# Denominators as extra columns of v, weight casts held behind the heads' norms, and three low parts on GpSimd

## The chip, the cores and the metric

The kernel runs on one core of a Trainium2 chip. The metric is the device time of one execution in microseconds. A profile of one execution is read beside it: the matmul engine (TensorE, PE), the vector engine (VectorE, DVE), the activation engine (ScalarE, ACT), GpSimd (POOL) and the queue that issues DMAs (SyncE, SP) are recorded instruction by instruction.

## The reference

Two layers of a decoder trunk on 256 tokens of width 1024. Each layer has a token mixer, a residual with layer norm, a SwiGLU channel mixer, a second residual with layer norm, and a gated embedding. Layer 0 mixes tokens with a gated spatial unit, layer 1 with an mLSTM block of 4 heads, each 512 wide. The change lies in layer 1. What matters of it:

```python
q, k = headwise_linear(xc, w_q), headwise_linear(xc, w_k)
v = headwise_linear(xm, w_v)
...
s = einsum('bhtd,bhsd->bhts', qb, kb) * exp(dmat - m_t[..., None])
num = einsum('bhts,bhsd->bhtd', s, vb) + ...
den = sum(s, axis=-1) + ...
h = num / maximum(abs(den), exp(-m_t))[..., None]
...
h = layer_norm(h, norm_g).reshape(B, S, ML_INNER) + skip * xc
return (h * silu(z)) @ w_out
```

So each head needs its weighted sum of v, the plain sum of its scores (the denominator), a division, and a layer norm over its 512 columns. The result is scaled, added to a skip path, gated by silu(z) and multiplied by the output weights.

## The kernel before

**Two parts for each number.** All products run in a reduced fp32 format, and each operand is split in a high part (a rounded copy) and a low part (the rest). A product is then three matmuls: high by high, low by high, high by low. `split` (L150) makes the parts: ScalarE copies the high one, and `sub`, VectorE unless the call says GpSimd, subtracts for the low one.

**Weights.** They stream from HBM in blocks of 128x1024 in the order of a list. `ahead` (L169 on) issues loads into four "raw" buffers and casts raw blocks into six "w" buffers, two instructions a block, so many blocks ahead of the block in use. A raw buffer is free again when both parts are made. The output weights are the blocks ("mo", 0) to ("mo", 15). `behind["cast"]` holds instructions that later casts are to be ordered behind: `issue_after` puts such an order only between instructions of the same engine, as an order in that engine's queue and not as a wait on another engine.

**Order of the work.** A planner puts each engine's instructions in an order before the run: of those that are ready by its own estimate, the one that comes first in the program. At run time each engine takes its queue strictly in that order. Only the ScalarE instructions of the gate stage stand in program order, by hand.

**The mLSTM stage.** Every head h has four blocks of 128 features. First come the products for xm, q and v (L754 to L797); v goes, in two parts, into one buffer `vn[h]` (L726, L796). Then scores (L801 to L824), then gates and exponentials, which end in the weights of the sums, `phi` (high) and `plo` (low, made on GpSimd), for every head (L896 to L914). Because of causality a head has three 128x128 blocks of them: one for the first 128 tokens, two for the second 128.

Then `pv_block(h)` (L923): nine matmuls of 512 columns add up the weighted sum for both token halves in two PSUM banks of pool A (`num`), and six matmuls against ones, two columns each, add up the denominators in a bank of pool B (`pd`). Each pool has four banks. VectorE forms 1/max(|den|, .) (L944 to L948), statistics of num (L952, L953), the variance (L956); GpSimd raises it to -1/2 (L957, "pow"); VectorE makes the scale and the shift, `nb` (L958, L960); ScalarE applies both while it reads num from PSUM (L962), and the banks are free.

`h_block(h)` (L967) transposes a head's result on TensorE and lets VectorE and ScalarE make its four features: scale and skip (L976), gate (L977), and the two parts.

The order in the program is: for each head, `pv_block`, then one block of z (24 matmuls of 256 columns); `h_block(0)` behind z of head 2; then `h_block(1)` and the product with the output weights. That product accumulates over 16 features into four banks of pool A, two for each token half (t = 0, 1). The first three features are taken together, all of t = 0 and then all of t = 1; later ones one by one.

## Time and profile before

| what | value |
|---|---|
| median of 3 runs | 823.44 us (823.26 to 823.69) |
| profiled execution | 823.71 us |
| its span in the trace | 822.0 us |
| TensorE matmul busy | 816.2 us (99%) |
| VectorE busy | 616.9 us (75%) |
| ScalarE busy | 471.8 us (57%) |
| GpSimd busy | 152.1 us (19%) |
| granted TensorE clock | 0.999 |

The heads' sums start at 535.1 us of the span and the product with the output weights at 559.0 us. A row of a timeline gives the start, the length (of several, if merged: x2), the engine, the line, the operation, what it writes and reads, and in brackets how long the engine stood idle before it and what ended that. A row of a view by stages gives the stretch and its length, then the busy time of the engine with the number of instructions in progress in it (those that began before the stretch too), the granted clock, the DMA share and the rate in GB/s. A row of waits gives who waited for whom: microseconds in total, times, longest. Row of a tile or line: durations in ns, least, median and most, first and last start.

### The profile page before, as it was taken

Reading aid. Unit: us, or ns where it says so; the run is one execution under the profiler, and the core shown is the slowest. Engines: PE = TensorE matmul, PEld = TensorE weight load, DVE = VectorE, ACT = ScalarE, POOL = GpSimd, SP = SyncE. Lnnn points to the kernel's source line nnn. Section 1 sums busy time; section 2 is a strip of 40 time slices with the busy share of each in tenths; the row PEclk is TensorE's granted clock in tenths of the full one; section 3 lists DMA queues with packets and bytes.
Section 4 is the critical chain, followed back from the end, with each engine's and each line's share of the span. In section 5 each row is a group of like instructions: output and inputs, shape, how many; then the busy total and the mean of one; then the engine's idle time right before and its main releaser. Section 6 shows DMA issues by size and latency. Waiting matters only on the chain.

```text
span 822.0 us, 12471 instructions
## 1 busy us (share of the span) xinstructions
PE 816.2 (99%) x4546; PEld 709.1 (86%) x4546; DVE 616.9 (75%) x985; ACT 471.8 (57%) x824; POOL 152.1 (19%) x209
## 2 busy tenths in 40 slices
PE   9999999999999999999999999999999999999997
PEld 6888888888888888888889999998888888888886
DVE  6667998678966567587878998889896566776674
ACT  6556666565554455465256788776544455665522
POOL 1120643343000000700001677430000000000000
PEclk9999999999999999999999999999999999999999
DMA  8885447558176668667144345453635667886501
GB/s 300 306 306 180 153 156 228 179 182 274 42 258 195 216 217 283 202 228 246 43 151 154 125 164 165 152 199 129 207 126 193 198 206 234 274 256 209 180 1 52
DMA packets 44998, 155.54 MB, mean 189 GB/s; under 512 B 5256, under 2 KB 6024, under 8 KB 44936
## 3 DMA queue, kind: packets, MB, share of 16 engines
q1 hardware_dynamic: 44504, 154.21, 57.2%
q8 instruction: 36, 0.59, 0.3%
q10 hardware_dynamic: 432, 0.52, 0.2%
q14 instruction: 26, 0.21, 0.1%
HBM read 153.67 MB, written 1.05 MB: 188 GB/s over the span
## 4 chain that ended last, share of the span: by engine, by line
PE 98%; DMA 1%; DVE 0%; ACTq 0%; ACT 0%; issue 0%; DVEq 0%
PE acc L238 9%; PE acc L239 9%; PE acc L240 9%; PE pu L258 9%; PE pg L258 9%; PE ups L258 5%; PE pg L262 5%; PE pu L262 5%; PE ups L262 3%; PE vps L240 2%; PE vps L238 2%; PE vps L239 2%; PE xmps L243 2%; PE xmps L244 2%; PE xmps L245 2%; PE gate L287 2%
## 5 line engine op out<-in xcount | busy, mean ns | idle before, releaser
L152 DVE TENSOR_TENSOR w<-raw,w 128x1024 fp32r<-128x1024 f32 (+1 forms) x275 | 333.1, 1219 | 70.1 <-ACT w L152 69.2
L152 ACT CAST w<-raw 128x1024 fp32r<-128x1024 f32 (+1 forms) x275 | 284.9, 1046 | 104.2 <-PE acc L240 23.4
L238 PE MATMUL acc<-w,h 128*128 128x512 f32 x336 | 133.0, 396 | 0.0
L239 PE MATMUL acc<-w,h 128*128 128x512 f32 x336 | 131.3, 391 | 0.0
L240 PE MATMUL acc<-w,h 128*128 128x512 f32 x336 | 131.0, 390 | 0.0
L258 PE MATMUL pu<-xs,w 128*128 128x512 f32 x320 | 79.4, 390 | 0.0
L258 PE MATMUL pg<-xs,w 128*128 128x512 f32 x320 | 79.3, 390 | 0.0
L240 PEld LDWEIGHTS acc<-w,h 128*128 128x128 f32 x336 | 63.1, 188 | 13.8
L238 PEld LDWEIGHTS acc<-w,h 128*128 128x128 f32 x336 | 63.1, 188 | 11.3
L239 PEld LDWEIGHTS acc<-w,h 128*128 128x128 f32 x336 | 63.2, 188 | 11.1
L258 PEld LDWEIGHTS pg<-xs,w 128*128 128x128 f32 x320 | 59.9, 188 | 12.4
L258 PEld LDWEIGHTS pu<-xs,w 128*128 128x128 f32 x320 | 59.8, 188 | 12.3
L269 ACT COPY s<-pg 128x256 f32<-128x256 f32 x40 | 14.9, 372 | 92.1 <-PE pg L262 92.1
L317 POOL TENSOR_TENSOR rs<-ve,mhalf 128x1 f32<-128x1 f32 x8 | 7.6, 954 | 296.7 <-DVE ve L316 251.8
L270 DVE TENSOR_TENSOR s<-s,pg 128x256 f32<-128x256 f32 x40 | 16.8, 420 | 60.7 <-ACT s L269 60.6
L258 PE MATMUL ups<-xs,w 128*128 128x512 f32 x192 | 47.9, 392 | 0.0
L262 PEld LDWEIGHTS pg<-xs,w 128*128 128x128 f32 x320 | 43.2, 188 | 3.4
L262 PE MATMUL pg<-xs,w 128*128 128x256 f32 x320 | 43.9, 280 | 0.0
L262 PE MATMUL pu<-xs,w 128*128 128x256 f32 x320 | 43.8, 279 | 0.0
L258 PEld LDWEIGHTS ups<-xs,w 128*128 128x128 f32 x192 | 35.7, 188 | 7.2
L262 PEld LDWEIGHTS pu<-xs,w 128*128 128x128 f32 x320 | 40.6, 188 | 0.3
L243 PE MATMUL xmps<-xs,w 128*128 128x256 f32 x128 | 36.3, 284 | 0.0
(251 smaller groups left out, 1587.0 us busy)
## 6 DMA issues: line engine op xcount, KB each, us to landing
raw<-in_ffn_d SPq DMA_DIRECT2D x44, 512.0 KB, 4.3
raw<-in_ffn_g SPq DMA_DIRECT2D x40, 512.0 KB, 4.3
raw<-in_ffn_u SPq DMA_DIRECT2D x40, 512.0 KB, 4.1
raw<-in_gm_u SPq DMA_DIRECT2D x24, 512.0 KB, 3.3
raw<-in_gm_wo SPq DMA_DIRECT2D x24, 512.0 KB, 3.3
raw<-in_gm_v SPq DMA_DIRECT2D x21, 512.0 KB, 5.2
raw<-in_ple_gate SPq DMA_DIRECT2D x16, 512.0 KB, 4.5
raw<-in_ml_z SPq DMA_DIRECT2D x16, 512.0 KB, 3.4
```

Source lines behind the costliest of these rows:

```text
L152: return dve.tensor_copy(hi, src) if fast else act.copy(hi, src), sub.tensor_tensor(lo, src, hi.bitcast(F32), ALU.subtract)
L238: pe.matmul(ps, lh, w[:, 0, c], start=start, stop=False)
L239: pe.matmul(ps, ll, w[:, 0, c], start=False, stop=False)
L240: pe.matmul(ps, lh, w[:, 1, c], start=False, stop=stop)
L243: pe.matmul(ps, w[:, 0, c], h, start=start, stop=False)
L244: pe.matmul(ps, w[:, 0, c], l, start=False, stop=False)
L245: pe.matmul(ps, w[:, 1, c], h, start=False, stop=stop)
L258: pe.matmul(ps, w[:, 0, k * P:(k + 1) * P], xs[:, k], start=k == 0, stop=False)
L262: pe.matmul(ps[:, 0], w[:, 1, k * P:(k + 1) * P], xh[:, k, :], start=False, stop=k == KD - 1)
L269: act.copy(o, ps[:, 1])
L270: dve.tensor_tensor(o, o, ps[:, 0], ALU.add)
L287: pe.matmul(ps, xl[:, k, TOK[t]], w[:, 0, c], start=False, stop=k == KD - 1)
```

## The change

- **Denominators.** `vn[h]` gets two columns of ones behind each 512 of its high part, made by GpSimd. The sums of a head go to three banks instead: the lower 256 columns of both token halves in one bank of pool A (`low`), the upper 256 with the ones behind them in one bank each (`top`), one of pool A and one of pool B. A block of scores takes four matmuls with its high part and two with its low part, of 256 or 258 columns. The six matmuls against ones are gone. The norm reads four pieces of 256 columns: two more small instructions for the denominator, four statistics, four reads by ScalarE.
- **Casts.** Output weight blocks 1, 2 and 3 have orders of their own: ScalarE's part behind the last exponential of head 3, GpSimd's behind the pow of head 1, 2 or 3. Blocks from 4 on are held behind `nb` of head 3 rather than its statistics.
- **GpSimd** makes the low parts of these three blocks.
- **Features.** Feature 3 of head 0 is held behind the variance of head 3. The transposes and features of head 1 move from before the output product to between its t = 0 and t = 1 of the first three features, and their VectorE part behind `nb` of head 3.
- **vsum**, the sum of the two parts of v, moves from the "cf" buffers to the "m2" buffers.

```diff
@@ -33,6 +33,8 @@
 
 LOAD_AHEAD = 8
 CAST_AHEAD = 4
+
+ON_POOL = (("mo", 1), ("mo", 2), ("mo", 3))
 HOLD = 4
 LAG = 2
 LAG_S = 3
@@ -189,7 +191,7 @@
                 step = D + ASIDE if paired(key) else D
                 t = tl("w", [P, 2 * D + P], F32R, "w")[:, first:first + 2 * step]
                 t = t.rearrange("p (i n) -> p i n", i=2)[:, :, :D]
-            with issue_after(behind["cast"]):
+            with issue_after(behind.get(key, behind["cast"])):
                 if key[0] == "bdv":
 
                     t = t.rearrange("p i n -> p (i n)")[:, :4 * 2 * GW].rearrange("p (j i n) -> p j i n", j=4, i=2)
@@ -197,7 +199,7 @@
                     f = 4 * key[1]
                     pool.tensor_copy(t[:, :, :, P:], wx[:, f:f + 4, :].rearrange("p j (i n) -> p j i n", i=2))
                 for c in () if key[0] == "bdv" else HALF if i < 3 else [slice(0, n)]:
-                    split(t[:, 0, c], t[:, 1, c], raw[:, c])
+                    split(t[:, 0, c], t[:, 1, c], raw[:, c], sub=pool if key in ON_POOL else dve)
             wt[i] = t
             at["cast"] += 1
 
@@ -723,7 +725,11 @@
             bdm[n] = bdm[n].rearrange("p i t n a -> p i (t n a)")
 
         block_diagonal(0)
-        vn = [tl("b8", [P, 2, 2, 512], F32R, "vn") for _ in range(NH)]
+
+
+        vn = [tl("b8", [P, 2 * D + P], F32R, "vn") for _ in range(NH)]
+        vh = [v[:, :1028].rearrange("p (s n) -> p s n", n=514) for v in vn]
+        vl = [v[:, D + P:].rearrange("p (s n) -> p s n", n=512) for v in vn]
         a1 = [tl("b8", [P, 8, S], name="a1") for _ in range(2)]
         sz = [tl("b8", [P, 8, S], name="sz") for _ in range(2)]
         sc = []
@@ -786,14 +792,16 @@
 
             m = bd["v"][:, j]
             c = slice(j * P, (j + 1) * P)
-            o = tl("cf", [P, 3 * P], name="vsum")[:, :2 * GW].rearrange("p (t n) -> p t n", t=2)
+            o = tl("m2", [P, 2 * GW], name="vsum").rearrange("p (t n) -> p t n", t=2)
             for t in range(2):
                 ps = bank("BA"[t], [P, 2, GW], "vps")
                 pe.matmul(ps, xm[:, 0, TOK[t]], m, start=True, stop=False)
                 pe.matmul(ps[:, 0], xm[:, 1, TOK[t]], m[:, 0], start=False, stop=True)
                 act.copy(o[:, t], ps[:, 0])
                 dve.tensor_tensor(o[:, t], o[:, t], ps[:, 1], ALU.add)
-            split(vn[h][:, 0, :, c], vn[h][:, 1, :, c], o[:, :, :P], sub=pool)
+            split(vh[h][:, :, c], vl[h][:, :, c], o[:, :, :P], sub=pool)
+            if j == 3:
+                pool.tensor_copy(vh[h][:, :, 512:], ones_r[:, :4].rearrange("p (s n) -> p s n", s=2))
             pool.tensor_tensor(gacc, gacc, o[:, :, P:], ALU.add)
 
         pss = []
@@ -903,7 +911,7 @@
                 e = tl("m2", [P, 384], name="e")
                 act.activation(e[:, 0:P], gm[:, 0, :], AF.Exp, bias=cols[:, 0, h:h + 1], scale=-1.0)
                 act.activation(e[:, P:S], gb[:, 1, :], AF.Exp, bias=cols[:, 0, h:h + 1], scale=-1.0)
-                act.activation(e[:, S:384], gm[:, 1, :], AF.Exp, bias=cols[:, 1, h:h + 1], scale=-1.0)
+                behind["exp"] = act.activation(e[:, S:384], gm[:, 1, :], AF.Exp, bias=cols[:, 1, h:h + 1], scale=-1.0)
                 if h == 1:
                     act.activation(cols[:, 2:4, :], cols[:, 2:4, :], AF.Exp, scale=-1.0)
                 p = sc[h]
@@ -922,47 +930,66 @@
 
         def pv_block(h):
             hi, lo = ph[h]
-            pd = bank("B", [P, 2, 2], "pd")
-            num = [bank("A", [P, 512], "num") for _ in range(2)]
+            halves = slice(0, 256), slice(256, 512)
+            low = bank("A", [P, 2, 256], "num")
+            top = [bank(w, [P, 258], "num") for w in "AB"]
+
+            den = [n[:, 256:257] for n in top]
+            num = [(low[:, t, :], top[t][:, :256]) for t in range(2)]
 
             for t, blocks in enumerate(BLOCKS):
                 for i, (s, c) in enumerate(blocks):
-                    pe.matmul(num[t], hi[:, c], vn[h][:, 0, s, :], start=i == 0, stop=False)
-                    pe.matmul(num[t], hi[:, c], vn[h][:, 1, s, :], start=False, stop=False)
+
+                    pe.matmul(low[:, t, :], hi[:, c], vh[h][:, s, :256], start=t == i == 0, stop=False)
+                    pe.matmul(top[t], hi[:, c], vh[h][:, s, 256:], start=i == 0, stop=False)
+                    for n, half in zip(num[t], halves):
+                        pe.matmul(n, hi[:, c], vl[h][:, s, half], start=False, stop=False)
             for t, blocks in enumerate(BLOCKS):
                 for i, (s, c) in enumerate(blocks):
-                    pe.matmul(num[t], lo[:, c], vn[h][:, 0, s, :], start=False, stop=i == len(blocks) - 1)
-
-            for t, (s, c) in DEN:
-                first, end = s == 0, s == t
-                pe.matmul(pd[:, t, :], hi[:, c], ones_r[:, :2], start=first, stop=False)
-                pe.matmul(pd[:, t, :], lo[:, c], ones_r[:, :2], start=False, stop=end)
+                    end = i == len(blocks) - 1
+                    pe.matmul(low[:, t, :], lo[:, c], vh[h][:, s, :256], start=False, stop=end and t == 1)
+                    pe.matmul(top[t], lo[:, c], vh[h][:, s, 256:], start=False, stop=end)
             o = tl("b8", [P, 2, 512], name="hn")
             hn.append(o)
 
             dn = tl("c", [P, 2], name="dn")
-            dve.scalar_tensor_tensor(dn, pd[:, :, 0], -1.0, cols[:, 2:4, h], ALU.mult, ALU.max)
-            dve.tensor_tensor(dn, dn, pd[:, :, 0], ALU.max)
+            for t in range(2):
+                dve.scalar_tensor_tensor(dn[:, t:t + 1], den[t], -1.0, cols[:, 2 + t, h:h + 1], ALU.mult, ALU.max)
+                dve.tensor_tensor(dn[:, t:t + 1], dn[:, t:t + 1], den[t], ALU.max)
             dve.reciprocal(dn, dn)
             dn2 = tl("c", [P, 2], name="dn2")
             dve.tensor_tensor(dn2, dn, dn, ALU.mult)
-            st = tl("c", [P, 2, 6], name="hst")
+            st = tl("c", [P, 2, 2, 6], name="hst")
             mv = tl("c", [P, 2, 2], name="hmv")
             for t in range(2):
-                end = dve.bn_stats(st[:, t, :], num[t])
-                dve.bn_aggr(mv[:, t, :], st[:, t, :])
+                for i in range(2):
+                    dve.bn_stats(st[:, t, i, :], num[t][i])
+                dve.bn_aggr(mv[:, t, :], st[:, t])
             rs = tl("c", [P, 2], name="hrs")
             for t in range(2):
-                dve.tensor_scalar(rs[:, t:t + 1], mv[:, t, 1:2], dn2[:, t:t + 1], EPS, ALU.mult, ALU.add)
-            pool.tensor_tensor(rs, rs, mhalf[:, :2], ALU.pow)
+                var = dve.tensor_scalar(rs[:, t:t + 1], mv[:, t, 1:2], dn2[:, t:t + 1], EPS, ALU.mult, ALU.add)
+
+            behind["mo", h] = behind["exp"], var, pool.tensor_tensor(rs, rs, mhalf[:, :2], ALU.pow)
             dve.tensor_tensor(rs, rs, dn, ALU.mult)
             nb = tl("c", [P, 2], name="nb")
-            dve.scalar_tensor_tensor(nb, mv[:, :, 0], -1.0, rs, ALU.mult, ALU.mult)
+            end = dve.scalar_tensor_tensor(nb, mv[:, :, 0], -1.0, rs, ALU.mult, ALU.mult)
+            if h == NH - 1:
+
+                behind["norm"] = end,
             for t in range(2):
-                act.activation(o[:, t, :], num[t], AF.Identity, bias=nb[:, t:t + 1], scale=rs[:, t:t + 1])
-            return (end,)
+                for n, half in zip(num[t], halves):
+                    act.activation(o[:, t, half], n, AF.Identity, bias=nb[:, t:t + 1], scale=rs[:, t:t + 1])
 
         hs = {}
+
+        def h_feature(f, tp):
+            y = tl("s", [P, S], name="y")
+            dve.scalar_tensor_tensor(y, tp, par[:, f, 6:7], a1[f // 8][:, f % 8, :], ALU.mult, ALU.add)
+            dve.tensor_tensor(y, y, sz[f // 8][:, f % 8, :], ALU.mult)
+            hs[f] = tl("h", [P, 2, S], F32R, "h")
+            split(hs[f][:, 0, :], hs[f][:, 1, :], y)
+
+        held = []
 
         def h_block(h):
             for j in range(2):
@@ -972,30 +999,33 @@
                         pe.transpose(tp[:, i, TOK[t]], hn[h][:, t, (2 * j + i) * P:(2 * j + i + 1) * P], ident)
                 for i in range(2):
                     f = 4 * h + 2 * j + i
-                    y = tl("s", [P, S], name="y")
-                    dve.scalar_tensor_tensor(y, tp[:, i, :], par[:, f, 6:7], a1[f // 8][:, f % 8, :], ALU.mult, ALU.add)
-                    dve.tensor_tensor(y, y, sz[f // 8][:, f % 8, :], ALU.mult)
-                    hs[f] = tl("h", [P, 2, S], F32R, "h")
-                    split(hs[f][:, 0, :], hs[f][:, 1, :], y)
+                    if f == 3:
+                        held.append((f, tp[:, i, :]))
+                    else:
+                        h_feature(f, tp[:, i, :])
 
         for h in range(NH):
             if h == NH - 1:
                 ahead(LOAD_AHEAD, 4)
-            end = pv_block(h)
+            pv_block(h)
             z_act(*z_mm(12 + h))
             if h == NH - 2:
                 h_block(0)
+        with issue_after(behind["mo", NH - 1]):
+            h_feature(*held.pop())
+        behind["mo", NH - 1] += behind["norm"]
         acc = Down(NI)
         begin = []
         for h in range(NH):
             if h == 2:
                 load_p(1)
-            if h + 1 < NH:
+            if h == 0:
+                ahead(LOAD_AHEAD, 4)
+            if 0 < h < NH - 1:
                 h_block(h + 1)
             for f in range(4 * h, 4 * h + 4):
                 if f == 1:
-
-                    behind["cast"] = end
+                    behind["cast"] = behind["norm"]
                 block = (f, hs.pop(f), weight("mo", f, casts=1 if f >= NI - 2 else None))
                 if f < 3:
 
@@ -1003,6 +1033,9 @@
                     for t in range(2) if f == 2 else ():
                         for b, h2, w in begin:
                             acc.mm(b, t, h2, w)
+                        if t == 0:
+                            with issue_after(behind["norm"]):
+                                h_block(1)
                 else:
                     acc.add(*block)
         return acc
```

## The prediction

> **What bounds the kernel now.** I read the page first, then the waits of TensorE, then the stages around the change in order of time.
>
> ```profile
> span 822.0 us, 12471 instructions
> ...
> PE 98%; DMA 1%; DVE 0%; ACTq 0%; ACT 0%; issue 0%; DVEq 0%
> ```
>
> The chain of work that ended last is TensorE for 98% of the span. These are all of its waits:
>
> ```profile
> PE warm L355 <- PEq L1096: 0.8, 1, 0.8
> PE vps L419 <- ACT xs L375: 0.5, 1, 0.5
> ```
>
> So 1.3 us of waiting, all at the start. From there TensorE runs without a stall: a product taken away shortens the kernel by its spacing, and any wait of TensorE lengthens it by its length.
>
> **What TensorE saves.** The view by stages, for head 0: first its nine products of 512 columns into num, then the six of two columns into pd with the first product of z, then the other 23 products of z (256 columns each).
>
> ```profile
> 535.10:537.18 2.08, 2.08 (x12) 1.00 0.87 282
> 537.18:537.96 0.78, 0.78 (x8) 1.00 0.80 299
> 537.96:540.67 2.71, 2.71 (x24) 1.00 0.90 310
> ```
>
> A product of 256 columns takes 2.71/23 = 0.118 us. The new head has 18 of 256 or 258 columns: for each of three blocks four with the high part of the scores and two with the low part. With the first product of z that makes 19 x 0.118 = 2.24 us where 2.08 + 0.78 = 2.86 us stand. Saved: 0.62 us a head, **2.5 us** for four. A 258-column product is not in the trace; between 0.118 and 0.118 x 258/256 it makes no difference. [...] The moved transposes of head 1 are as many as before, and on TensorE they cost what they cost there.
>
> **What GpSimd gets, and what it blocks.** Low parts of output blocks 1 to 3 leave VectorE, where one takes 1.2 us (548.15 below), for GpSimd. No op of 128x1024 of this kind is in the trace; nearest are these, on GpSimd:
>
> ```profile
> L152 POOL TENSOR_TENSOR vn<-vsum,vn x16: 723/735/1258, 460.0 to 521.6; 128x256 fp32r<-128x256 f32 x16
> ```
>
> ```profile
> 537.17 1.53 POOL L152 TENSOR_TENSOR plo<-sc,phi 128x384 fp32r<-128x384 f32 x1 [1.04 <-ACT phi L152]
> ...
> 542.22 1.01 POOL L152 TENSOR_TENSOR plo<-sc,phi 128x384 fp32r<-128x384 f32 x1 [1.04 <-ACT phi L152]
> 543.62 0.73 POOL L957 TENSOR_TENSOR hrs<-hrs,mhalf 128x2 f32<-128x2 f32 x1 [0.39 <-DVE hrs L956]
> ```
>
> From 0.73 us for 256 columns to 1.01 us for 384 is 0.28 per 128; 1024 columns give 1.01 + 5 x 0.28 = 2.4 us, or 2.7 in proportion to 384. I take 2.4. On VectorE at that time:
>
> ```profile
> 532.90 0.54 DVE L910 SCALAR_TENSOR_TENSOR sc<-sc,e 128x384 f32<-128x384 f32 x1
> ...
> 538.09 1.02 DVE L910 SCALAR_TENSOR_TENSOR sc<-sc,e 128x384 f32<-128x384 f32 x1
> ```
>
> L910 reads two SBUF tensors. It takes 0.54 us with GpSimd idle. The one of 538.09 meets the GpSimd op that runs to 537.17 + 1.53 = 538.70 and ends at 539.11, 0.41 later: it stood still until GpSimd was done. So a 2.4 us op on GpSimd stops VectorE's queue at its next op with two SBUF inputs. The trace shows this for wide ops alone, not for one of two columns. [...]
>
> **Where it falls.** The low part of block h is ordered behind L957 (pow) of head h, and nothing else stands in GpSimd's queue there. What VectorE does around a pow, for head 1:
>
> ```profile
> 544.38 0.16 DVE L958 TENSOR_TENSOR hrs<-hrs,dn 128x2 f32<-128x2 f32 x1 [0.84 <-POOL hrs L957]
> 544.58 0.16 DVE L960 SCALAR_TENSOR_TENSOR nb<-hmv,hrs 128x2 f32<-128x2 f32 x1
> 544.65 0.15 DVE L944 SCALAR_TENSOR_TENSOR dn<-pd,cols 128x2 f32<-128x2 f32 x1
> 544.84 0.16 DVE L945 TENSOR_TENSOR dn<-dn,pd 128x2 f32<-128x2 f32 x1
> 545.03 0.17 DVE L946 RECIPROCAL dn<-dn 128x2 f32<-128x2 f32 x1
> 545.23 0.16 DVE L948 TENSOR_TENSOR dn<-dn 128x2 f32<-128x2 f32 x1
> 545.31 1.29 DVE L952 BATCH_NORM_STATS2 hst<-num 128x6 f32<-128x512 f32 x2
> 546.52 0.30 DVE L953 BATCH_NORM_AGGREGATE hmv<-hst 128x2 f32<-128x6 f32 x2
> 546.73 0.33 DVE L956 TENSOR_SCALAR hrs<-hmv,dn 128x1 f32<-128x1 f32 x2
> 547.88 0.16 DVE L958 TENSOR_TENSOR hrs<-hrs,dn 128x2 f32<-128x2 f32 x1 [0.81 <-POOL hrs L957]
> 548.07 0.16 DVE L960 SCALAR_TENSOR_TENSOR nb<-hmv,hrs 128x2 f32<-128x2 f32 x1
> 548.15 1.23 DVE L152 TENSOR_TENSOR w<-raw,w 128x1024 fp32r<-128x1024 f32 x1
> ```
>
> L958 starts 0.03 us after the pow that ends at 543.62 + 0.73; L960 follows 0.2 us later. Both read two SBUF tensors. The high part of the block is made by ScalarE behind head 3's exponentials alone, so it is ready long before; GpSimd goes straight from the pow into the 2.4 us, and L960, which gives the norm's shift (nb), waits for it. Everything behind L960 on VectorE waits too.
>
> A norm, from L944 to the end of L956, is 544.65 to 547.06, 2.41 us. New: two more small ops (0.08 to 0.19 us each by the starts above, 0.27 in all), and statistics of four 256-column pieces. Two of 512 take 546.52 - 545.31 = 1.21; a two-column op occupies 0.08, so four halves take 4 x (0.08 + (0.605 - 0.08)/2) = 1.37, 0.16 more (bounds 0 and 1.21). The norm is then 2.84 us.
>
> The chain on VectorE, nothing else changed ahead of it: head 1 from 544.65, L956 done 547.49, L958 0.82 later at 548.3, L960 after 2.4 at 550.7. Head 2 the same from there: 550.8 + 2.84 + 0.82 + 2.4 = 556.9. Then features 0 to 2:
>
> ```profile
> 554.05 0.15 DVE L960 SCALAR_TENSOR_TENSOR nb<-hmv,hrs 128x2 f32<-128x2 f32 x1
> 554.11 0.75 DVE L977 TENSOR_TENSOR y<-y,sz 128x256 f32<-128x256 f32 x2
> 554.78 0.87 DVE L976 SCALAR_TENSOR_TENSOR y<-tp,par,a 128x256 f32<-128x256 f32 x2
> ...
> 561.84 0.15 DVE L960 SCALAR_TENSOR_TENSOR nb<-hmv,hrs 128x2 f32<-128x2 f32 x1
> ```
>
> By these spacings (L977 0.34, L976 0.39; the low parts as L977) three L977, one L976 and three low parts are 2.4 us; the held feature 3 is out of the way, in the gap behind head 3's L956. Head 3: 556.9 + 2.4 + 2.84 + 0.82 + 2.4 = 565.4, where 561.84 stands. The three 1.2 us casts that left VectorE are counted by being absent here.
>
> **Why that reaches TensorE.** The accumulator of the output product needs all four A banks; its second half (t = 1) takes those of head 3, when ScalarE (L962) has read them.
>
> ```profile
> 544.96 1.44 ACT L962 ACTIVATE hn<-num,nb,hrs 128x512 f32<-128x512 f32 x2
> ...
> 562.09 1.45 ACT L962 ACTIVATE hn<-num,nb,hrs 128x512 f32<-128x512 f32 x2 [0.86 <-DVE nb L960]
> ```
>
> ```profile
> 546.21 0.39 PE L930 MATMUL num<-vn,phi 128*128 128x512 f32 x1
> ...
> 559.02 0.48 PE L238 MATMUL acc<-w,h 128*128 128x512 f32 x1
> ```
>
> ```profile
> 563.20 0.39 PE L238 MATMUL acc<-w,h 128*128 128x512 f32 x1
> ```
>
> The accumulator starts at 559.02, 18 products later t = 1 at 563.20, and its first bank was free after the first of the two L962, half of 1.45 us after 562.09, near 562.85: only 0.35 us to spare. TensorE will be there 2.5 us sooner, at 560.7 (the transposes of head 1 go from before the first half to before the second, which leaves this point where it was). ScalarE starts 0.25 us after L960, and the first A bank is free after two of the new 256-column reads. One takes between 0.36 us, half of a 512-column read, and the whole 0.72; I take 0.4, since these ops have mostly gone by columns above, and 0.8 for two: t = 1 starts at 565.4 + 1.05 = 566.4, **3.2 us later** than now. This is the upper end. The lower end fills VectorE's idle 0.8 us behind a pow with the next head's first small ops, which TensorE now delivers early enough at two of the heads: 3.2 - 1.6 = 1.6 us. VectorE's idle gaps in the rows above have no ready work today, so I take a value nearer to the lower end, **1.9 us later**. Later stages have their work behind TensorE and shift with it.
>
> **Edits that cost nothing.** Moving vsum to the m2 buffers and four copies of ones on GpSimd lie in the stage before, under TensorE's stream; four columns are under the 0.73 us of 256, so 2.9 us in all bounds it uncovered. GpSimd holds a raw block until its low part is done, so the loads of blocks 5 to 7 start later, the last one near 565. From 559.02 to 563.20, 18 products take 4.2 us, a block (12) 2.8; block 5 is due 4.2 + 2 x 2.8 us behind t = 1, near 573, block 7 near 579, and the loads have these 8 us and more.
>
> The sum: the profiled execution took 823.71 us (its span 822.0 and 1.7 around it), so 825.6 by it; the median of the three runs is 823.44, 0.27 below, and gives **825.3 us**.
>
> **Rivals.** A: the lock does not stop two-column ops, or L960 slips through. Then heads 1 to 3 end 2.4 us sooner each: head 3's nb at 565.4 - 7.2 = 558.2, its first A bank at 559.3, before TensorE's 560.7, so t = 1 does not wait. What is late next is head 2's first product: TensorE is there at 546.21 - 1.25 = 544.96, just as ScalarE starts reading head 0's banks, and the second bank is free three reads (1.15 us) later: 0.5 to 1.0 us lost, less if ScalarE is sooner. 823.44 - 2.5 + 0.8 = **821.7 us**, not slower. For it: no row shows a small op blocked. Against it: L910's rows. B: one of the three low parts does no harm, block 1's, whose cast on ScalarE is the last in rank of what waits there, so that it starts behind L960 of head 1. Then nb of head 3 is at 565.4 - 2.4 = 563.0, less up to 1.6 for filled gaps, t = 1 at 562.5 to 564.1, 0.7 before to 0.9 behind now: **823.5 us**. Against it: ScalarE sits idle ahead of several of the ops shown, time enough for a cast. C: nothing fills a gap, and TensorE besides waits for B banks, which the held feature 3 and the upper half of each head's sums now keep; that wait lies under the one at t = 1, so the upper end decides, 823.44 + 3.2 = **826.6 us**.
>
> **How the numbers follow.** A measurement of this kernel tells 0.2% (1.65 us) from no change. Forecast 0.42 (its own range 824.7 to 826.2; 0.34 of it slower, 0.08 within), A 0.33 (0.25 faster, 0.08 within), B 0.18 (0.02 faster, 0.16 within), C 0.07 (0.06 slower, 0.01 within). Faster 0.27, same 0.33, slower 0.40. The range reaches over A's better part to the upper end: 821.3 to 826.7.
>
> **What would show it.** Each step has a row: numerators and z of a head in 4.95 us on TensorE; GpSimd's 128x1024 ops starting where a pow ends and lasting 2.4 us; L960 ending with them; t = 1 of the accumulator late and a wait of TensorE for ScalarE's L962 there. If L960 starts 0.2 us behind L958 while GpSimd runs, the lock step is wrong and A holds. If no wait of TensorE appears from 535 to 570, the saving stands whole, at 821.

## The result, and the profile after

The changed kernel takes **829.94 us** (median of 5 executions, 828.27 to 830.38) where the kernel before takes 823.58 on the same chip (5 executions, 823.26 to 823.89): 1.0072 times as long, 95% interval 1.0061 to 1.0082. That is 6.4 us more, and outside the forecast range of 821.3 to 826.7. The profiled execution took 830.38 us with a span of 828.6. Two of the five executions, 828.27 and 828.50 us, ran at a mean granted clock of 1.0, the other three, the profiled one among them, at 0.997 to 0.998, for a reason told below.

The page of the changed kernel: the span, and the chain of work that ended last, by engine.

```profile
span 828.6 us, 12537 instructions
...
PE 31%; DVE 2%; issue 2%; POOL 1%; ACT 1%; DVEq 0%; POOLq 0%; ACTq 0%
```

The chain was TensorE for 98% before. Now it can be followed through TensorE for 31% of the span only, back into a stage where other engines set the time. Which stage that is, the waits of TensorE between 530 and 620 us show (who waits for whom: total us, times, longest); the kernel before has none there:

```profile
PE acc L240 <- ACT hn L981: 2.0, 1, 2.0
PE tp L999 <- ACT hn L981: 1.5, 1, 1.5
PE zps L245 <- DVE y L987: 0.8, 1, 0.8
PE num L944 <- ACT sz L750: 0.8, 1, 0.8
PE num L943 <- ACT hn L981: 0.5, 1, 0.5
```

Together 5.6 us. The saving on TensorE itself is as forecast. By stages, head 0: its 18 products, then 24 of z.

```profile
535.46:537.61 2.15, 2.15 (x21) 2.15 (x19) 1.34 (x2) 0.79 (x4) 1.11 (x2) 1.00 1.00 389
537.61:540.43 2.82, 2.82 (x26) 2.82 (x25) 2.42 (x11) 2.13 (x8) 1.78 (x2) 1.00 0.89 344
```

4.97 us, where 4.95 was forecast and 5.57 stood before. What undoes it is GpSimd (timeline of GpSimd, head 1):

```profile
547.74 0.70 POOL L972 TENSOR_TENSOR hrs<-hrs,mhalf 128x2 f32<-128x2 f32 x1 [3.10 <-DVE hrs L970]
548.40 2.39 POOL L154 TENSOR_TENSOR w<-raw,w 128x1024 fp32r<-128x1024 f32 x1
```

and in the same stage VectorE (heads 1, 2 and 3):

```profile
548.48 2.33 DVE L973 TENSOR_TENSOR hrs<-hrs,dn 128x2 f32<-128x2 f32 x1 [0.82 <-POOL hrs L972]
550.84 0.16 DVE L975 SCALAR_TENSOR_TENSOR nb<-hmv,hrs 128x2 f32<-128x2 f32 x1
...
554.68 2.33 DVE L973 TENSOR_TENSOR hrs<-hrs,dn 128x2 f32<-128x2 f32 x1 [0.87 <-POOL hrs L972]
557.05 0.16 DVE L975 SCALAR_TENSOR_TENSOR nb<-hmv,hrs 128x2 f32<-128x2 f32 x1
...
564.01 2.33 DVE L973 TENSOR_TENSOR hrs<-hrs,dn 128x2 f32<-128x2 f32 x1 [0.41 <-POOL hrs L972]
566.27 0.41 DVE L988 TENSOR_TENSOR y<-y,sz 128x256 f32<-128x256 f32 x1
566.60 0.15 DVE L975 SCALAR_TENSOR_TENSOR nb<-hmv,hrs 128x2 f32<-128x2 f32 x1
```

L973 multiplies 128x2 numbers. It took 0.16 us before (as L958) and takes 2.33 us three times, each time until GpSimd's operation ends (at head 1: 548.40 + 2.39 = 550.79; 548.48 + 2.33 = 550.81; at heads 2 and 3 GpSimd's starts at 554.61 and 563.94 and takes 2.38 and 2.39 us). This stop is what the prediction and the expectations call the lock. The low part cost VectorE 1.2 us; handing it to GpSimd costs VectorE 2.2 us. ScalarE and TensorE behind head 3, each from its own timeline:

```profile
566.77 0.41 ACT L154 CAST h<-y 128x256 fp32r<-128x256 f32 x1 [4.23 <-DVE nb L975]
567.08 1.93 ACT L981 ACTIVATE hn<-num,nb,hrs 128x256 f32<-128x256 f32 x4
```

```profile
568.15 0.50 PE L240 MATMUL acc<-w,h 128*128 128x512 f32 x1 [2.00 <-ACT hn L981]
```

The second half (t = 1) of the accumulator starts at 568.15 instead of 563.20: **4.95 us later**. And TensorE then runs slowly for a while. By stages (the column after the five engines is the granted clock):

```profile
568.00:570.00 2.00, 1.85 (x7) 1.45 (x8) 2.00 (x4) 1.01 (x3) 0.00 (x0) 0.83 0.83 283
570.00:572.00 2.00, 2.00 (x6) 1.59 (x5) 2.00 (x7) 1.49 (x3) 0.00 (x0) 0.50 0.88 281
572.00:575.00 3.00, 3.00 (x13) 2.42 (x12) 2.63 (x6) 2.73 (x5) 0.00 (x0) 0.87 0.42 146
```

At a clock of 0.50 six products are in progress in 2 us, where the 18 products from 559.02 to 563.20 before, 0.23 us apart, would make nine. The stage costs some 1.7 us (0.17 x 2 + 0.50 x 2 + 0.13 x 3 = 1.73 us of clock not granted). 4.95 + 1.7 = 6.65 us, and the span grew by 6.6.

### The profile page after: what moved, and what is told of

Same layout as the page of the kernel before. It is cut to its first block, busy times and chain, and to the rows that moved or that the text cites. A ratio compares the mean times of both kernels' runs of the same rounds, so it can differ in the third digit from the quotient of the medians.

```text
span 828.6 us, 12537 instructions
## 1 busy us (share of the span) xinstructions
PE 817.7 (99%) x4558; PEld 710.4 (86%) x4558; DVE 622.1 (75%) x998; ACT 473.9 (57%) x832; POOL 159.5 (19%) x216
## 3 DMA queue, kind: packets, MB, share of 16 engines
HBM read 153.67 MB, written 1.05 MB: 187 GB/s over the span
## 5 line engine op out<-in xcount | busy, mean ns | idle before, releaser
L154 DVE TENSOR_TENSOR w<-raw,w 128x1024 fp32r<-128x1024 f32 (+1 forms) x272 | 329.6, 1219 | 72.2 <-ACT w L154 70.6
L476 POOL TENSOR_TENSOR sv<-sv,cf 128x256 f32<-128x256 f32 x22 | 23.3, 1060 | 71.0 <-ACT sv L475 71.0
```

The lines of the kernel that those rows point to most:

```text
L154: return dve.tensor_copy(hi, src) if fast else act.copy(hi, src), sub.tensor_tensor(lo, src, hi.bitcast(F32), ALU.subtract)
L476: pool.tensor_tensor(sv, sv, cf, ALU.add)
```

## The experiments

Runs on the chip beside the kernel before, whose medians were 823.40 to 823.49 us in the four groups (14 to 25 executions each). Line numbers of the variants differ by a few from those of the changed kernel.

### The blocks alone, and everything but the blocks

`e2_only_gpsimd`: the kernel before with one thing added, the three low parts on GpSimd and the orders that place them there.

```diff
-            with issue_after(behind["cast"]):
+            with issue_after(behind.get(key, behind["cast"])):
...
-                    split(t[:, 0, c], t[:, 1, c], raw[:, c])
+                    split(t[:, 0, c], t[:, 1, c], raw[:, c], sub=pool if key in ON_POOL else dve)
...
-            pool.tensor_tensor(rs, rs, mhalf[:, :2], ALU.pow)
+            behind["mo", h] = behind["exp"], pool.tensor_tensor(rs, rs, mhalf[:, :2], ALU.pow)
```

> The kernel before with one part of the change alone: low parts of output blocks 1 to 3 on GpSimd behind the pow of heads 1 to 3. Lock theory: three stops of 2.33 us in the chain of norms against two casts of 1.2 us that leave it, head 3's nb about 4.5 us later with 0.35 us to spare: 826.5 to 829.5 us. Longer norms: the norms are as before and VectorE is relieved of 3.6 us, 823 to 823.6 us.

Measured 829.92 us (829.27 to 830.72), ratio 1.0079 (1.0064 to 1.0094). Three operations moved to GpSimd, at these places, bring the whole loss with no other part of the change. It is a little above the theory's range, and TensorE's waits and stages say why:

```profile
PE acc L239 <- ACT hn L963: 4.3, 1, 4.3
```

```profile
566.00:568.00 2.00, 0.46 (x1) 0.47 (x2) 2.00 (x8) 1.29 (x2) 0.13 (x1) 0.50 0.39 129
```

One wait of 4.3 us, and behind it the half-speed stage, here the longer one: the clock stays at 0.50 until 572 us.

`e1_low_on_vector`: the changed kernel with all low parts on VectorE.

```diff
-ON_POOL = (("mo", 1), ("mo", 2), ("mo", 3))
+ON_POOL = ()
```

> The changed kernel with the three low parts back on VectorE, everything else kept. Lock theory (a GpSimd op of two SBUF inputs stops VectorE's L973 for its whole 2.33 us): behind each L970 of heads 1 to 3 stand 1.21 us of cast instead of 0.82 + 2.33 us of pow and lock, 1.7 us less three times, so head 3's nb comes 5 us sooner and the half-speed stage goes with the long wait: 822.5 to 824.5 us. Rival, longer norms (four statistics, four reads by ScalarE, sums that keep a B bank): GpSimd is not the cause, 828 to 830 us as the changed kernel.

824.21 us (823.67 to 825.45), ratio 1.0008 (0.9998 to 1.0018): no loss that can be told, and no gain. The stop works the other way here. VectorE's cast and, in a second view, GpSimd's pow of head 1:

```profile
547.71 1.22 DVE L154 TENSOR_TENSOR w<-raw,w 128x1024 fp32r<-128x1024 f32 x1
```

```profile
547.87 1.62 POOL L972 TENSOR_TENSOR hrs<-hrs,mhalf 128x2 f32<-128x2 f32 x1 [3.10 <-DVE hrs L970]
```

A pow of 0.70 us takes 1.62. So this norm still loses 0.9 us, in place of 2.2; those of heads 0 and 2 lose as much (1.64 and 1.60 us), that of head 3 nothing (0.69 us). The trace before had a sign of it: `plo` on GpSimd took 1.53 us at 537.17, while VectorE cast a block from 536.59 on (1.23 us), and 1.01 us at 542.22.

`e4_sums_alone`: only the denominators in v (and vsum in the "m2" buffers); no holds, no GpSimd blocks, the features in the order of before.

```diff
-                    if f == 3:
-                        held.append((f, tp[:, i, :]))
...
+                    h_feature(f, tp[:, i, :])
...
-            if h == 0:
-                ahead(LOAD_AHEAD, 4)
-            if 0 < h < NH - 1:
+            if h + 1 < NH:
```

> The kernel before with the denominators as columns of v alone (three sum banks, four-piece norm); casts on VectorE, feature 3 and head 1's features where they were before. Lock theory: TensorE saves 2.5 us, the norms are 0.4 us longer each with no lock, so the first bank of t = 1 is free near where it was and part of the saving shows: 822 to 824 us. Longer norms: 826 us and more.

824.45 us (824.10 to 824.97), ratio 1.0012 (1.0003 to 1.0022), just above the range. 2.5 us of products are gone and no time is saved; this question comes back below.

### What exactly stops VectorE

Three variants keep an operation of GpSimd at this place and change what it meets or what it reads. `e3_one_input` writes the norm's small products so that the second factor is a column given as a scalar, not a second tensor:

```diff
-            dve.tensor_tensor(rs, rs, dn, ALU.mult)
+            for t in range(2):
+                dve.tensor_scalar(rs[:, t:t + 1], rs[:, t:t + 1], dn[:, t:t + 1], None, ALU.mult)
```

> The changed kernel, but the three small VectorE ops of a norm that read two SBUF tensors (L961, L973, L975) become ops with one tensor and a column as scalar, two each; GpSimd keeps its three low parts. Lock theory, as told of ops with two SBUF inputs: nothing of a norm waits for GpSimd's 2.4 us any more, head 3's nb near 560, waits of TensorE under 1.5 us: 821 to 823 us. If the lock stops any VectorE op, or the longer norms are the cause: 828 to 830 us.

824.48 us (823.85 to 826.09), ratio 1.0012 (1.0003 to 1.0021), against 829.94 with GpSimd's work unchanged; that lies between the theory's 821 to 823 and the rival's 828 to 830. GpSimd, then VectorE, at head 3:

```profile
560.65 2.39 POOL L154 TENSOR_TENSOR w<-raw,w 128x1024 fp32r<-128x1024 f32 x1
```

```profile
560.72 0.34 DVE L975 TENSOR_SCALAR hrs<-hrs,dn 128x1 f32<-128x1 f32 x2 [0.48 <-POOL hrs L973]
560.98 0.34 DVE L978 TENSOR_SCALAR nb<-hmv,hrs 128x1 f32<-128x1 f32 x2
561.23 2.10 DVE L991 TENSOR_TENSOR y<-y,sz 128x256 f32<-128x256 f32 x1
```

The norm runs through GpSimd's 2.39 us. The next operation with two tensors in SBUF (L991, otherwise 0.41) stands until it ends. So VectorE as a whole is not stopped: the operations that ran read one tensor and a column, the one that stood reads two tensors in SBUF.

`e5_one_tensor_low` lets GpSimd read one tensor:

```diff
-                    split(t[:, 0, c], t[:, 1, c], raw[:, c], sub=pool if key in ON_POOL else dve)
+                    if key in ON_POOL:
+                        act.copy(t[:, 0, c], raw[:, c])
+                        pool.tensor_scalar(t[:, 1, c], raw[:, c], 0.0, None, ALU.mult)
```

> The changed kernel, but GpSimd's operation on output blocks 1 to 3 reads one tensor instead of two (the loaded block times zero, written to the same low part at the same place in the order); the low parts of these three blocks are thereby left out of the result. Lock theory: what stops VectorE is a GpSimd operation with two inputs in SBUF, so a one-tensor operation of the same 128x1024 leaves VectorE's short products behind pow alone (they end within 0.5 us of pow's end): 823.5 to 825.0 us, as with the low parts on VectorE or the one-input norm. Rival, any long operation of GpSimd at this place stops VectorE, or delays ScalarE or the loads: 828 to 831 us.

`e10_memset` lets it read nothing:

```diff
-                    split(t[:, 0, c], t[:, 1, c], raw[:, c], sub=pool if key in ON_POOL else dve)
+                    if key in ON_POOL:
+                        act.copy(t[:, 0, c], raw[:, c])
+                        pool.memset(t[:, 1, c].bitcast(F32), 0.0)
```

> The changed kernel, but in place of the low parts of output blocks 1 to 3 GpSimd sets the tile to zero, at the same place in the order: the operation reads nothing, and VectorE does not make these parts either (they are left out of the result). Lock theory: without an input GpSimd's operation does not stop VectorE; VectorE's short products behind pow run through (0.16 us instead of 2.33, or of the 1.0 that a one-tensor operation left); VectorE is also rid of 3.6 us of casts, so TensorE's 2.4 us show at last: 820.8 to 822.8 us. Rival, any 128x1024 operation of GpSimd stops VectorE: 825 to 830 us. If the products run through and the time is still 823.3 or more, VectorE's queue is not what eats the gain.

`e5_one_tensor_low`: 826.09 us (825.13 to 826.57), ratio 1.0031 (1.0018 to 1.0044), between the two expectations. GpSimd and VectorE at head 1:

```profile
548.10 2.78 POOL L204 TENSOR_SCALAR w<-raw 128x1024 fp32r<-128x1024 f32 x1
```

```profile
548.16 0.99 DVE L977 TENSOR_TENSOR hrs<-hrs,dn 128x2 f32<-128x2 f32 x1 [0.82 <-POOL hrs L976]
```

VectorE is stopped for 0.8 us of GpSimd's 2.78, not for all of it (at heads 2 and 3 L977 takes 1.00 and 0.99 us). `e10_memset`: 822.93 us (822.67 to 823.17), ratio 0.9993 (0.9984 to 1.0002).

```profile
548.13 0.96 POOL L204 MEMSET w<- 128x1024 f32 x1
```

```profile
548.22 0.16 DVE L977 TENSOR_TENSOR hrs<-hrs,dn 128x2 f32<-128x2 f32 x1 [0.82 <-POOL hrs L976]
```

The operation that only writes did not stop it. The three together: 2.33, 0.99 and 0.16 us for the same small product, with two, one and no tensor read by GpSimd. With the second factor as a column it ran beside two (0.34 us for two, in `e3_one_input`). Why `e5_one_tensor_low` lost 1.9 us more than `e1_low_on_vector`, although it stops VectorE for about as long (0.83 us) as that one stretches the pow (0.92 us), was not settled: its waits of TensorE lie partly behind the stage (0.7 us for ScalarE's xs).

### Which of the three blocks costs what

`e7_last_block` leaves block 3 alone on GpSimd (first line with a plus), `e8_first_two` the other two (second).

```diff
-ON_POOL = (("mo", 1), ("mo", 2), ("mo", 3))
+ON_POOL = (("mo", 3),)
...
+ON_POOL = (("mo", 1), ("mo", 2))
```

> The changed kernel with only output block 3's low part on GpSimd (behind head 3's power), blocks 1 and 2 on VectorE. Theory, that the holds of heads 1 and 2 push head 3's numerators out and so add to that of head 3: this one keeps head 3's hold alone, some 1.5 us later than with all low parts on VectorE (2.3 us stopped instead of the 0.9 us by which VectorE's own cast stretches the power), 825.2 to 826.5 us. Rival, the prediction's: only the last hold decides, since the waits ahead lie under the accumulator's wait: 827.5 to 830 us.

> The changed kernel with output blocks 1's and 2's low parts on GpSimd (behind heads 1's and 2's powers), block 3's on VectorE. Theory, that these holds push head 3's numerators out: TensorE's waits for the B banks (transposes 1.5 us, z 0.8 us, numerators 0.8 us) stay, and with them about 3 us over the kernel with all low parts on VectorE: 826.3 to 828.0 us. Rival, the prediction's: these waits lie under the accumulator's wait and are nearly free without the last hold: 824.0 to 825.2 us.

825.37 us (825.24 to 826.93), ratio 1.0026 (1.0016 to 1.0035), and 827.15 us (826.33 to 828.01), ratio 1.0046 (1.0031 to 1.0061): both inside the first theory's ranges, both outside the prediction's. The longest wait of TensorE, first of `e7_last_block`, then of `e8_first_two`:

```profile
PE acc L240 <- ACT hn L981: 1.7, 1, 1.7
```

```profile
PE tp L999 <- ACT hn L981: 1.4, 1, 1.4
```

Over `e1_low_on_vector` (824.21) the last block costs 1.2 us and the first two 2.9 us, together 4.1. The changed kernel costs 5.7 over it, and 4.2 in its two executions at full clock (828.4). So the stops of the three heads add up, as far as intervals of 0.8 to 1.2 us either way can tell, and the 1.6 us that are left have the size of the half-speed stage (1.73 us in the profiled execution).

### Is it the standing still that costs the clock?

`e6_bridge` and `e13_bridge_single` fill the wait ahead of t = 1 with products, in the changed kernel and in `e2_only_gpsimd`, where it is the only wait.

```diff
+                        for _ in range(EXTRA if t == 0 else 0):
+                            b, h2, w = begin[1]
+                            acc.mm(b, t, h2, w)
```

> The changed kernel with the six products of output block 1's first token half issued a second time, ahead of the accumulator's wait for its second half (1.4 us of added products in the 2.0 us wait; the first half's sums are thereby wrong). Theory, that the half-speed stage behind t=1 comes from TensorE standing still there: the wait falls to about 0.6 us, the products behind it stay 0.23 us apart, 828.0 to 828.9 us although there is more work. Rival, the clock falls for the shorter waits ahead of it or for another reason: the stage at 0.50 stays and the time is 829.5 to 831.5 us.

> The kernel of e2_only_gpsimd (before, with the three low parts on GpSimd), with the six products of output block 1's first token half issued three more times ahead of the accumulator's second half (4.1 us of added products in a wait of 4.3 us; the first half's sums are thereby wrong). Theory, that the clock falls because TensorE stands still in that wait: no product behind it runs at half speed, and 829.9 us fall to 827.4 to 828.6 us although there is 4.1 us more work. Rival, the clock has another cause: a stage below 0.9 stays and the time is 829.5 us or more.

The stages behind t = 1, of `e6_bridge` and of `e13_bridge_single`:

```profile
570.00:572.00 2.00, 2.00 (x11) 1.65 (x10) 1.12 (x3) 0.17 (x1) 0.00 (x0) 1.00 0.90 283
```

```profile
568.00:570.00 2.00, 2.00 (x10) 1.56 (x9) 1.92 (x6) 1.42 (x4) 0.00 (x0) 1.00 0.56 209
```

In both profiled executions the half-speed stage is gone. `e13_bridge_single` takes 828.79 us (828.29 to 829.36), 1.1 us less than `e2_only_gpsimd` with 4.1 us more work: it is 0.2 above the theory's upper end and below the rival's 829.5. `e6_bridge` had 828.76 us in the profiled execution, as the theory asked, but a median of 829.71 (828.76 to 830.07), which is in the rival's range: its other executions were not profiled, and their clocks of 0.999 to 1.0 do not show where they lost a microsecond. For one wait the cause is shown; for the changed kernel it rests on its profile and on the two executions at full clock.

The runs do not give one length of a wait behind which the clock falls. It fell behind 4.3 us in `e2_only_gpsimd` and behind 2.0 us in the changed kernel. `e11_pool_behind_nb`, below, has one wait of 3.7 us and a stage at 0.50 behind it; `e14_head0_cast` has one of 1.5 us and a stage at 0.55. But `e7_last_block` has one of 1.7 us, `e9_vector_behind_norm` one of 1.5 us and `e12_one_block_free` one of 1.8 us, and none of the three shows a slow stage in its profiled execution.

### Where the saved 2.5 us go

`e10_memset` has no stop behind the pows of heads 1 to 3 and is rid of three casts, and still gains only 0.5 us (its interval takes in no change). TensorE, the first products of heads 0 to 3 and of the output product:

```profile
535.19 0.28 PE L947 MATMUL num<-vn,phi 128*128 128x256 f32 x1
...
540.17 0.28 PE L947 MATMUL num<-vn,phi 128*128 128x256 f32 x1
...
546.16 0.39 PE L947 MATMUL num<-vn,phi 128*128 128x256 f32 x1 [0.48 <-ACT hn L985]
...
552.04 0.36 PE L947 MATMUL num<-vn,phi 128*128 128x256 f32 x1
...
557.58 0.39 PE L244 MATMUL acc<-w,h 128*128 128x512 f32 x1
```

Heads 0 to 3 take 4.98, 5.99, 5.09 (5.88 less 0.79 for the transposes between) and 5.54 us: 21.6 against 4 x 4.97 = 19.9 and against 4 x 5.57 = 22.3 before. So 1.7 us of the 2.4 are lost again, 1.0 at head 1, 0.1 at head 2 and 0.6 at head 3. The list of TensorE's waits shows 0.7 of it; those of its weight loads, which stand ahead of the products, show 1.4 (0.3, 0.7 and 0.4 us), each until ScalarE has read a bank. Before, TensorE had no wait in this stage. Two stops are left at head 0. By its own order, which the change gives to block 0 as well, that block's cast on VectorE falls on head 0's pow (1.64 us instead of 0.73); and then GpSimd's `plo` of another head stops L977 (GpSimd, then VectorE):

```profile
543.37 1.01 POOL L154 TENSOR_TENSOR plo<-sc,phi 128x384 fp32r<-128x384 f32 x1
```

```profile
543.43 0.97 DVE L977 TENSOR_TENSOR hrs<-hrs,dn 128x2 f32<-128x2 f32 x1 [0.62 <-POOL hrs L976]
```

Four attempts to free the banks sooner:

`e9_vector_behind_norm` has `ON_POOL = ()` and

```diff
-            behind["mo", h] = behind["exp"], var, pool.tensor_tensor(rs, rs, mhalf[:, :2], ALU.pow)
+            pool.tensor_tensor(rs, rs, mhalf[:, :2], ALU.pow)
...
+            behind["mo", h] = behind["exp"], end
...
-            for t in range(2):
-                for n, half in zip(num[t], halves):
-                    act.activation(o[:, t, half], n, AF.Identity, bias=nb[:, t:t + 1], scale=rs[:, t:t + 1])
+            for i, half in enumerate(halves):
+                for t in range(2):
+                    act.activation(o[:, t, half], num[t][i], AF.Identity, bias=nb[:, t:t + 1], scale=rs[:, t:t + 1])
```

`e11_pool_behind_nb` has the first two of these hunks with the blocks on GpSimd. `e12_one_block_free` leaves block 1 alone on GpSimd, has the third hunk, the products of `e3_one_input`, and (`pw` is the pow)

```diff
+                end = dve.tensor_scalar(nb[:, t:t + 1], mv[:, t, 0:1], -1.0, rs[:, t:t + 1], ALU.mult, ALU.mult)
+            behind["mo", h] = (behind["exp"], var, pw) if ("mo", h) in ON_POOL else (behind["exp"], end)
```

`e14_head0_cast` is `e10_memset` with

```diff
+            behind["mo", h] = (behind["exp"], var, pw) if h else (behind["exp"], end)
```

> The changed kernel with all low parts on VectorE, and those of output blocks 0 to 3 held behind the end of their head's norm instead of behind its power; ScalarE reads the bank of the lower halves first. Theory, that with no GpSimd block the rest of the gain is eaten because VectorE's cast stretches the power (1.6 us instead of 0.7) and so each norm by 0.9 us: the powers fall to 0.7 us, TensorE's waits in the numerators (2.1 us by the start-to-start distances) shrink to under 1 us, 822.3 to 823.6 us. Rival, that VectorE's queue as a whole is the bound (4.2 to 4.9 us busy in each 5 us): a cast moved behind the norm delays the next norm instead, 823.8 to 825.5 us.

> The changed kernel with the three low parts still on GpSimd, but held behind the end of the head's norm instead of behind its power. Lock theory: the norm's own products run through, and VectorE stops at the next operation with two inputs in SBUF, for heads 2 and 3 the products of the features (as with the one-input norm, where they took 1.7 and 2.1 us): 823.8 to 826.0 us. Rival, the holds cost the same wherever they fall, since VectorE's queue has no slack: 827 to 830 us.

> The changed kernel with the norm's three small products given as one-tensor operations with a column as the other factor, output block 1's low part alone on GpSimd behind head 1's power (where VectorE has no features to make yet), blocks 2 and 3 on VectorE behind the ends of their norms, ScalarE reading the lower halves first. Lock theory: GpSimd's block meets no VectorE operation with two inputs in SBUF and so costs nothing, and takes 1.2 us off VectorE: 821.8 to 823.3 us. Rival, VectorE's queue and the weights' casts bound what follows: 823.5 to 825.0 us.

> e10_memset (GpSimd sets the low parts of output blocks 1 to 3 to zero; these parts are left out of the result) with block 0's cast on VectorE held behind the end of head 0's norm, so that head 0's power takes 0.7 instead of 1.6 us. Theory, that TensorE's saved time waits for the banks which head 0's norm frees late: the wait at head 2's first product (0.5 us) goes and 822.0 to 822.6 us come out. Rival, the cast then delays head 1's norm and the wait moves to another bank: 822.7 to 823.5 us.

| kernel | median us (range) | ratio (interval) | longest wait of TensorE, 530 to 640 us |
|---|---|---|---|
| e9_vector_behind_norm | 825.33 (824.33 to 826.36) | 1.0023 (1.0012 to 1.0033) | 1.5, num |
| e11_pool_behind_nb | 828.71 (828.45 to 829.06) | 1.0062 (1.0049 to 1.0075) | 3.7, num |
| e12_one_block_free | 826.24 (824.74 to 828.56) | 1.0033 (1.0021 to 1.0046) | 1.8, acc |
| e14_head0_cast | 824.21 (823.29 to 825.39) | 1.0009 (1.0000 to 1.0018) | 1.5, num |

All four missed what the first theory expected. `e9_vector_behind_norm` and `e11_pool_behind_nb` lie in the ranges of their rivals, the other two above both ranges; none of the four decides the question, since more changed than was meant. `e14_head0_cast` shows what happens. Head 0's pow does fall to 0.7 us, so its shift is ready earlier, and the planner puts ScalarE's other work between the reads of the banks. ScalarE at head 0, and TensorE's stage behind it:

```profile
543.25 0.57 ACT L986 ACTIVATE hn<-num,nb,hrs 128x256 f32<-128x256 f32 x1 [1.21 <-DVE nb L979]
543.83 1.28 ACT L928 ACT_TABLE_LOAD   x1
...
546.08 1.46 ACT L986 ACTIVATE hn<-num,nb,hrs 128x256 f32<-128x256 f32 x3
```

```profile
548.00:551.00 3.00, 3.00 (x17) 3.00 (x17) 1.23 (x8) 2.81 (x6) 0.60 (x1) 0.55 0.03 5
```

The first read is done at 543.8, the other three come behind a table load and the gate of 1024 columns, and head 2's first product waits 1.5 instead of 0.5 us; the clock falls on top, in some executions: five of the ten took 823.3 to 823.7 us at a clock of 0.998 to 1.0, the other five 824.8 to 825.4 at 0.996 to 0.997. The first five alone would lie at the upper end of the rival's range. `e9_vector_behind_norm` has the same order of ScalarE. `e11_pool_behind_nb` did not test what it was made for. Its order names VectorE's `nb`, and as an order holds only between instructions of the same engine, it does not hold GpSimd at all. GpSimd's first block came right behind head 0's pow, at 542.68; the other two came in a row at 554.30, so that head 2's L961 (`dn` times itself, 128x2) took 2.25 us from 554.45 on, and its pow waited for both. Its question stays open, but it gives a third kernel with a long wait (3.7 us, for the banks of head 0) and the slow stage behind it (GpSimd's first block, and the stage):

```profile
542.68 2.40 POOL L154 TENSOR_TENSOR w<-raw,w 128x1024 fp32r<-128x1024 f32 x1
```

```profile
550.00:552.00 2.00, 2.00 (x11) 2.00 (x11) 0.32 (x2) 1.64 (x5) 0.59 (x1) 0.50 0.11 35
```

In `e12_one_block_free` no wait up to t = 1 is above 0.55 us, and the longest one, 1.8 us, comes at 599 us, for ScalarE's cast of an output weight block. That points to the loads. `e15_no_holds` is `e1_low_on_vector` without the holds of blocks 0 to 3.

```diff
-            with issue_after(behind.get(key, behind["cast"])):
+            with issue_after(behind["cast"]):
```

> The changed kernel with all low parts on VectorE and without the holds on output blocks 0 to 3, so that each is cast when its load has landed, as before; the sums in v and head 1's features behind the last norm stay. Theory, that the holds push ScalarE's casts and the loads behind them back (ScalarE waited 7.8 us for the output weights after the stage in e1_low_on_vector, 3.8 before): 822.3 to 823.4 us. Rival, VectorE's queue in the stage is what eats the gain, with or without holds: 823.8 to 825.0 us.

823.72 us (823.22 to 824.12), ratio 1.0001 (0.9992 to 1.0010), between the two ranges. ScalarE's waits for loads of output weights from 575 to 612 us, of the kernel before, of `e1_low_on_vector` and of `e15_no_holds`:

```profile
ACT w L152 <- DMA raw<-in_ml_wo: 3.8, 3, 2.8
```

```profile
ACT w L154 <- DMA raw<-in_ml_wo: 7.8, 4, 4.0
```

```profile
ACT w L154 <- DMA raw<-in_ml_wo: 3.7, 4, 1.7
```

Without the holds ScalarE waits for loads as little as before. In time that is some 0.4 us (0.32 over its group's kernel before, against 0.72 for `e1_low_on_vector`), and the intervals overlap, so the cost of the holds is likely, not shown. No variant is faster than the kernel before by more than a measurement can tell.

## Why the prediction was wrong

That GpSimd's operation stops VectorE, and that this reaches TensorE at t = 1, was right. The step that turned it into a time failed, the upper end of the estimate was too low as well, and one effect was missing.

- **TensorE's saving**: 4.97 us a head for 4.95 forecast. Right.
- **GpSimd's operation**: 2.39 us for 2.4 forecast, starting where the pow ends. Right. It stops L973 already, where the forecast let this product (as L958) through and stopped only `nb` behind it; `nb` comes at the same time either way. That the stop holds for an operation of two columns was the prediction's assumption, which the trace before could not show; it was settled by 2.33 against 0.16 us. Rival A, which rests on the opposite, fell; rival B too: all three blocks stop VectorE.
- **The step that failed: "I take a value nearer to the lower end, 1.9 us later"** for t = 1, on the ground that the next head's first small operations, "which TensorE now delivers early enough at two of the heads", would fill VectorE's idle gap behind a pow. It is 4.95 us. No gap was filled behind heads 1 and 2: `nb` came at 550.84 and 557.05, where the upper chain, with no gap filled, had 550.7 and 556.9. And TensorE did not deliver early: it was waiting itself. VectorE stood idle from 547.66 to 548.48 and from 553.81 to 554.68; the last numerator product of head 2 and the first of head 3 are these:

```profile
548.55 0.28 PE L951 MATMUL num<-vn,plo 128*128 128x258 f32 x1
...
553.94 0.36 PE L943 MATMUL num<-vn,phi 128*128 128x256 f32 x1
```

So there was next to nothing ready to fill a gap with; whether the order of VectorE's queue would have let it pass is not shown. TensorE came to t = 1 at 566.15 (565.12 + 1.03), not at 560.7, and only the last 2.00 of the 4.95 us are the wait there. That rival C, which has no gap filled, got a chance of 0.07 was the misjudgement.

- **The upper end was itself too low**, 566.4 against 568.15. Head 3's `nb` came 1.2 us behind the forecast 565.4: three scale-and-skip operations and not one lie between heads 2 and 3 (2 x 0.39 us), and the held feature's gate (0.33 us) stands between L973 and `nb`. From `nb` to t = 1 it is 1.55 us for 1.05: the four reads of 256 columns take 1.93 us, so that the first two are done 1.07 us after their start and not 0.8, and a cast of 0.3 us comes ahead of them.
- **"That wait lies under the one at t = 1"** (rival C, of the B banks) is wrong. `e8_first_two` has those waits without the last hold and takes 827.15 us, 2.9 more than without any GpSimd block. The waits of TensorE ahead delay head 3's numerators, and so the last norm: its `nb` comes at 563.70 there, against 561.59 in `e1_low_on_vector`.
- **Not foreseen**: the half-speed stage, some 1.7 us where it occurs. The trace before could not show it: TensorE's longest wait there is 0.8 us, at the start.
- **"Edits that cost nothing"** was half right: the delayed loads are not free without the larger losses (7.8 against 3.8 us of ScalarE's waits for them), but in the result they hardly count. Its 573 us for block 5 counts from the 563.20 of before; from the forecast's own t = 1 it would be 575.
- **Rival A's 821.7 us without a stop** was too good by about 1.2 us: `e10_memset`, without a stop at heads 1 to 3, is at 822.93 although VectorE is rid of their casts altogether. Of the 2.4 us saved, 1.7 are lost again, at least 1.4 of them to banks that are freed too late, where 0.5 to 1.0 was allowed for.

## What to carry to other kernels

Before moving an operation to GpSimd, look at what VectorE does during it: here both read two tensors in SBUF, VectorE's product took 2.33 us instead of 0.16, until GpSimd's operation of 2.39 us ended, and 1.2 us handed over cost 2.2. An engine that is at 98% of the chain gains from less work only if what frees its buffers runs ahead of it by more than the gain; the start-to-start distances of its stages show that better than the list of its waits. And holding one instruction back changes the planned order of other engines too: in `e9_vector_behind_norm` and `e14_head0_cast` that made TensorE's longest wait 1.5 us, where it was 0.6 and 0.5 us.

## What the runs showed of the hardware

- A VectorE product of 128x2 with two SBUF tensors took 2.33, 0.99 and 0.16 us beside a GpSimd operation of 128x1024 that read two, one and no tensors; beside a shorter one that read two tensors (128x384, 1.01 us) it took 0.97 us. With its second factor as a column it took 0.34 us for two beside the first kind. The other way round, GpSimd's pow took 1.62 us beside a VectorE cast of 1.22 us, and 0.70 us without one.
- TensorE's granted clock fell to 0.50 for a few microseconds behind waits of 4.3 and 3.7 us, and, in some executions, to 0.50 and 0.55 behind waits of 2.0 and 1.5 us; behind waits of 1.8, 1.7 and 1.5 us in other kernels the profiled execution shows no fall. With the wait of 4.3 us filled by products the clock stayed at 1.00: 4.1 us of added work made that kernel 1.1 us faster.
